# Quarter sums by block transposes and small products, in place of four full transposes, in layer 0 of a two-layer diffusion backbone

## The chip, the cores and the metric

The kernel runs on one core of a Trainium2 chip. The metric is the device time of one execution in microseconds; a time given for a kernel is the median of its runs.

## What is computed

Two layers of a diffusion backbone work on 256 latent tokens and 256 context tokens of width 2048. Layer 0 mixes tokens by centred pooling, layer 1 by neighbourhood attention; each is followed by a gated MLP of width 5504. Every sub-layer is normalised and then shifted, scaled and gated by vectors that come out of the conditioning:

```python
    silu_c, silu_cc = jax.nn.silu(c), jax.nn.silu(c_ctx)
    for i in range(DEPTH):
        ml = (silu_c @ w_mod[i] + b_mod[i]).reshape(B, 6, 1, D)
        mc = (silu_cc @ w_mod[i] + b_mod[i]).reshape(6, 1, 1, D)
        a_lat = modulate(rms_norm(h, norm1_g[i]), ml[:, 0], ml[:, 1])
        a_ctx = modulate(rms_norm(hc, norm1_g[i]), mc[0], mc[1])
        ...
        h = h + ml[:, 2] * y_lat
        h = h + ml[:, 5] * conv_ffn(modulate(rms_norm(h, norm2_g[i]), ml[:, 3], ml[:, 4]), ...)
```

`modulate(x, shift, scale)` is `x * (1 + scale) + shift`. The two streams, latent and context, are two columns beside each other wherever a vector of the conditioning is meant.

## The kernel before

Channels lie on the partitions, tokens along the free dimension, both streams beside each other (512 columns). Most products are in fp32r, with weights and activations split into a high and a low part, so that three products stand for one; those of the conditioning are plain fp32. The instructions are written in an order, and a scheduler with a simulated timeline then orders each engine's queue, by readiness and by the written order as priority; `tc.high_priority()` lifts what is written under it above its place. Each engine's queue is in order on the chip.

The conditioning of layer 0 (the modulation) is 24 chunks of 512 output channels. A chunk is the function `mod_pe`: in four steps it loads 1 MB of weights each, and multiplies them with the conditioning. The stationary operand is 32 columns wide (two hold the streams, the rest are zero), and four such products stand side by side in the column groups of the array (`tile_position`), each with another quarter of the contraction, into one PSUM bank, tag "m", of which there is one (L193). So the bank ends up with four partial sums, at partitions 0, 32, 64 and 96, two rows each, along 512 columns. They have to be added, and turned so that the channels lie on the partitions. Before, ScalarE copies the bank to SBUF (L198, "modev"), TensorE turns it by four full 128x128 transposes (L203, "modt", under high priority), and VectorE adds the four quarters with one reduction (L205); `by_row` is the view for that. `finish_mod` adds the bias (L181) and, for a scale, multiplies (L183).

The generator `mods` runs through the chunks, and `need(n)` drives it to step n. Between the steps, the mixer of the pooling layer and the early part of the MLP are written: `partial(g, ...)` multiplies the MLP's gate and up weights of the first eight blocks with the channel group g as soon as that group is through the mixer, on activations without the shift (L545 to L547). The part of the shift goes through the same weights separately: `pw` (L528) multiplies the unsplit weights with the shift `sh`, again with 32 columns in four column groups, in 16 units (four channel groups, two blocks of four, gate and up). Its bank is copied by ScalarE (L532, "peg" and "peu"), turned by four transposes (L561, "ptg" and "ptu") at the end of the unit, and reduced (L564, or L568 and an addition L569) into `wsh`.

`quad` is a matrix that sums four quarters of the partitions; layer 1's conditioning uses it in `quarter_sum` (L165), behind VectorE's block transposes (L251), which turn each 32x32 block of a tile in its place. Loads are issued on SP's queue into a ring of rooms of half a megabyte (L127); a room comes free when the last reader of its weights is done. The tiles of 512 columns share a ring of six, tag "t2"; PSUM banks of tag "d" are three.

Of the kernel before, what the change touches and what calls it, by code (L numbers as in the profile page):

```python
# [17 lines left out]
P = 128  # L18
# [39 lines left out]
def kernel(ctx: ExitStack, tc: tile.TileContext, xT, cxT, wmod, wg, wu, wd, wp,  # L58
# [10 lines left out]
    def bank(tag, name):  # L69

        if tag == "d" and nbank[0] is not None:
            nbank[0] += 1
            if nbank[0] % 4 == 0:
                tag = "m"
        return pp.tile([P, 512], F32, tag=tag, bufs={"gu": 4, "d": 3, "m": 1}[tag], name=name)
# [78 lines left out]

    both = (0, 1)

    def by_row(ps):

        return ps.rearrange("p (i j c) -> p i c j", i=4, j=4)[:, :, 0:2, :]

    def quarter_sum(x, n, name):

# [5 lines left out]

    def finish_mod(l, ch, streams, src):

        mt = src[0] if len(src) == 1 else main.tile([P, 4, 2], F32, name=f"modT{l}_{ch}")
        n = len(streams)
        which, q = divmod(ch, 4)

        def dup(name, a):
            return V(name)[:, a : a + 8].rearrange("p (i s) -> p i s", s=2)[:, :, 0:n]

        bias = dup(f"bm_{l}", 8 * ch)
        for b, v in enumerate(src):
            own = slice(32 * b, 32 * b + 32) if len(src) > 1 else slice(0, P)  # L180
            nc.vector.tensor_tensor(mt[own, :, 0:n], v, bias[own], op=ALU.add)  # L181
        if which in (1, 4):
            nc.vector.scalar_tensor_tensor(mt[:, :, 0:n], mt[:, :, 0:n], 1.0, dup(f"g{1 if which == 1 else 2}_{l}", 8 * q),  # L183
                                           op0=ALU.add, op1=ALU.mult)
        modT[l, ch] = mt

    def mod_pe(l, ch, sc, pool):

        ps = bank("m", f"mod{l}_{ch}")
        for g in range(4):  # L190
            ts = load(lambda a, b: wmod[l, ch, g, :, a:b], 2048, f"wm{l}_{ch}_{g}")
            for j in range(4):
                nc.tensor.matmul(ps[32 * j : 32 * j + 32, :], sc[:, 4 * g + j, :],  # L193
                                 ts[j // 2][0][:, 512 * (j % 2) : 512 * (j % 2) + 512],
                                 start=(g == 0), stop=(g == 3), tile_position=(0, 32 * j))
            if g == 3:
                ev = pool.tile([P, 512], F32, tag="t2", name=f"modev{l}_{ch}")
                nc.scalar.copy(ev, ps)  # L198
            yield
        with tc.high_priority():  # L200
            p2 = bank("d", f"modt{l}_{ch}")
            for i in range(4):
                nc.tensor.transpose(p2[:, P * i : P * i + P], ev[:, P * i : P * i + P], ident)  # L203
        r = main.tile([P, 4, 2], F32, name=f"modT{l}_{ch}")
        nc.vector.tensor_reduce(out=r, in_=by_row(p2), axis=AX.X, op=ALU.add)  # L205
        finish_mod(l, ch, both, [r])

    def mod_pairs(todo, ring):

# [113 lines left out]
    with ExitStack() as ph0:  # L323
# [62 lines left out]
        with ExitStack() as phs:  # L386
# [123 lines left out]
            def partial(g, sh, between):  # L510

                step = 0
                for fa in range(0, NS, 4):
                    for q, (nm, wsrc) in enumerate((("g", wg), ("u", wu))):
# [3 lines left out]
                        for j in range(4):  # L518
                            f = fa + j
                            between(2 * step)  # L520
                            if j == (3 if fa == 0 and q == 0 else 0):
                                need(20 * g + 21)
                                assert g in READY
                                pw = bank("d", f"pw{nm}{g}_{fa}")
                                for i in range(4):
                                    for jj, (t, n) in enumerate(ts):
                                        t3 = t.rearrange("p (f c) -> p f c", c=512)
                                        nc.tensor.matmul(pw[32 * i : 32 * i + 32, 256 * jj : 256 * jj + 256], sh[:, i, :],  # L528
                                                         t3[:, :, P * i : P * i + P], start=True, stop=True,
                                                         tile_position=(0, 32 * i))  # L530
                                ev = f0.tile([P, 512], F32, tag="t2", name=f"pe{nm}{g}_{fa}")
                                nc.scalar.copy(ev, pw)  # L532
                            if f >= NC:
                                if g == 0:
                                    HELD[f, q] = bank("gu", f"c{nm}_{f}")
# [20 lines left out]
                                nc.scalar.copy(PART[f][:, q], ps)  # L556
                            else:
                                nc.vector.tensor_tensor(PART[f][:, q], PART[f][:, q], ps, op=ALU.add)
                        p2 = bank("d", f"pt{nm}{g}_{fa}")
                        for i in range(4):  # L560
                            nc.tensor.transpose(p2[:, P * i : P * i + P], ev[:, P * i : P * i + P], ident)  # L561
                        w_ = wsh[:, q, fa : fa + 4, :]
                        if g == 0:
                            nc.vector.tensor_reduce(out=w_, in_=by_row(p2), axis=AX.X, op=ALU.add)  # L564
                            continue
                        t_ = f0.tile([P, 512], F32, tag="t2", name=f"pu{nm}{g}_{fa}")[:, 0:8]
                        t_ = t_.rearrange("p (f s) -> p f s", s=2)
                        nc.vector.tensor_reduce(out=t_, in_=by_row(p2), axis=AX.X, op=ALU.add)  # L568
                        nc.vector.tensor_tensor(w_, w_, t_, op=ALU.add)  # L569
            lend(range(4, KT))  # L570
            mix = mixer(0)
            for n in STEPS:
# [659 lines left out]
```

## Time and profile before

| | us |
|---|---|
| median of 3 runs | 3101.84 |
| lowest and highest | 3100.47, 3102.82 |
| the profiled execution | 3103.48 |
| its span, first to last instruction | 3101.7 |
| TensorE busy in the span | 3030.0 |
| VectorE busy | 1932.6 |
| ScalarE busy | 1373.2 |
| GpSimd busy | 826.1 |

The profile comes from one execution of its own, so its times are compared with that execution's. In its rows PE is TensorE's matmuls, PEld its weight loads, which overlap with them, DVE VectorE, ACT ScalarE, POOL GpSimd and SPq the queue that issues the loads. Matmuls overlap, so that their durations can't be added; the distance from start to start says what one takes of the engine. The early part that the change touches lies in the first 455 us.

### The profile page before, as it was taken

The page shows a single profiled execution, that of the slowest core. Times are in us where ns is not written, and L with a number is a line of the kernel's source. Part 1 is how long each engine was busy: PE and PEld are TensorE (multiplying, and loading weights), DVE is VectorE, ACT ScalarE, POOL GpSimd, SP SyncE. Part 2 cuts the span into 40 slices and gives each one's busy share as a digit, 9 for nine tenths or more (in the row PEclk, how much of TensorE's full clock was granted, in tenths as well). Part 3 has the DMA queues.
Part 4 walks back from the last instruction along what each step waited for, and adds up shares of the span by engine and source line. Part 5 has one row for each costly group of instructions (what it writes and reads, how often), then busy time and mean ns, then how long its engine had stood idle before and what let it go on. Part 6 is the DMA issues. An engine that isn't in the chain of part 4 may idle for free.

```text
span 3101.7 us, 40819 instructions
## 1 busy us (share of the span) xinstructions
PE 3030.0 (98%) x15082; PEld 2414.3 (78%) x15082; DVE 1932.6 (62%) x2748; ACT 1373.2 (44%) x2219; POOL 826.1 (27%) x823
## 2 busy tenths in 40 slices
PE   6999899999999999999999999999999999999998
PEld 2565558888888888888888788878788888888887
DVE  4445674285765848567485665564777666666666
ACT  3333454333233332323334444343545666656665
POOL 2011213213031230302213000000002466556665
PEclk9999999999999999999999999999999999999999
DMA  9978573264846657475573333332345565555563
GB/s 376 333 271 306 177 246 102 89 217 149 251 141 206 198 162 247 133 225 171 182 226 118 102 113 106 102 114 96 111 153 179 177 196 188 192 189 185 179 195 117
DMA packets 177927, 559.70 MB, mean 180 GB/s; under 512 B 17600, under 2 KB 22208, under 8 KB 177728
## 3 DMA queue, kind: packets, MB, share of 16 engines
q1 hardware_dynamic: 177728, 557.10, 55.0%
q8 instruction: 119, 1.95, 0.3%
q14 instruction: 80, 0.66, 0.1%
HBM read 554.93 MB, written 2.10 MB: 180 GB/s over the span
## 4 chain that ended last, share of the span: by engine, by line
PE 94%; DMA 2%; DVE 2%; POOL 1%; ACT 1%; issue 0%; SPq 0%; DVEq 0%; ACTq 0%; POOLq 0%
PE g L766 5%; PE u L766 5%; PE d L657 5%; PE d L659 5%; PE d L658 5%; PE d L813 4%; PE u L631 4%; PE u L632 4%; PE u L633 4%; PE g L631 4%; PE g L633 4%; PE g L632 4%; PE mod L193 3%; PE u L769 3%; PE g L769 3%; PE d L817 2%
## 5 line engine op out<-in xcount | busy, mean ns | idle before, releaser
L670 POOL TENSOR_TENSOR hl<-hl,dy 128x256 f32<-128x256 f32 x160 | 149.0, 931 | 958.6 <-ACT dy L669 957.3
L828 POOL TENSOR_TENSOR hl<-hl,dy 128x256 f32<-128x256 f32 x320 | 331.5, 1069 | 188.4 <-ACT dy L826 186.1
L241 DVE SCALAR_TENSOR_TENSOR macc<-wm,sc,macc 128x512 f32<-128x512 f32 (+1 forms) x360 | 325.2, 935 | 68.6 <-DMA wm<-wmod 67.6
L669 ACT ACTIVATE dy<-d,modT 128x256 f32<-128x256 f32 x320 | 133.5, 470 | 196.8 <-PE d L659 195.5
L193 PE MATMUL mod<-wm,sc 128*32 128x512 f32 x768 | 134.6, 618 | 26.6 <-DMA wm<-wmod 26.5
L670 POOL TENSOR_TENSOR hc<-hc,dy 128x256 f32<-128x256 f32 x160 | 126.0, 787 | 0.0
L145 DVE TENSOR_TENSOR wd_2l<-wd,wd_2h 128x1024 fp32r<-128x1024 f32 (+1 forms) x44 | 53.9, 1229 | 112.8 <-ACT wd_2h L143 112.8
L826 ACT ACTIVATE dy<-d,modT 128x512 f32<-128x512 f32 x160 | 104.4, 683 | 42.7 <-PE d L817 41.2
L915 POOL TENSOR_TENSOR rk<-rk,rp 128x256 f32<-128x256 f32 x16 | 13.2, 826 | 365.4 <-DVE rk L914 309.8
L145 DVE TENSOR_TENSOR wd_3l<-wd,wd_3h 128x1024 fp32r<-128x1024 f32 (+1 forms) x44 | 52.0, 1202 | 80.6 <-ACT wd_3h L143 80.6
L145 DVE TENSOR_TENSOR wd_1l<-wd,wd_1h 128x1024 fp32r<-128x1024 f32 (+1 forms) x44 | 53.7, 1224 | 58.6 <-ACT wd_1h L143 58.6
L466 POOL TENSOR_TENSOR pf<-ws,inv 128x256 f32<-128x256 f32 x32 | 27.7, 886 | 222.4 <-DVE ws L461 154.7
L193 PEld LDWEIGHTS mod<-wm,sc 128*32 128x32 f32 x768 | 23.6, 110 | 81.0 <-issue 59.4
L143 ACT CAST wd_1h<-wd 128x1024 fp32r<-128x1024 f32 (+1 forms) x44 | 45.2, 1029 | 79.8 <-PE u L632 50.6
L145 DVE TENSOR_TENSOR wd_0l<-wd,wd_0h 128x1024 fp32r<-128x1024 f32 (+1 forms) x44 | 54.6, 1247 | 40.7 <-ACT wd_0h L143 40.6
L1004 ACT ACTIVATE sb<-sb,nm 128x512 f32<-128x512 f32 x64 | 46.1, 721 | 64.4 <-DVE nm L1000 63.2
L143 ACT CAST wd_0h<-wd 128x1024 fp32r<-128x1024 f32 (+1 forms) x44 | 45.3, 1031 | 57.9 <-PE u L766 29.1
L792 DVE TENSOR_TENSOR actb<-sgb,actb 128x256 fp32r<-128x256 f32 x43 | 52.3, 1216 | 27.0 <-ACT actb L791 27.0
L657 PE MATMUL d<-act,wd_2h 128*128 128x512 f32 x172 | 68.0, 395 | 0.0
L658 PE MATMUL d<-act,wd_2h 128*128 128x512 f32 x172 | 67.9, 395 | 0.0
L657 PE MATMUL d<-act,wd_3h 128*128 128x512 f32 x172 | 67.9, 395 | 0.0
L657 PE MATMUL d<-act,wd_0h 128*128 128x512 f32 x172 | 67.9, 395 | 0.0
(1752 smaller groups left out, 9286.1 us busy)
## 6 DMA issues: line engine op xcount, KB each, us to landing
wm<-wmod SPq DMA_DIRECT2D x384, 512.0 KB, 6.1
wd<-wd SPq DMA_DIRECT2D x168, 512.0 KB, 4.4
wg<-wg SPq DMA_DIRECT2D x156, 512.0 KB, 4.6
wu<-wu SPq DMA_DIRECT2D x156, 512.0 KB, 4.5
wv<-wv SPq DMA_DIRECT2D x32, 512.0 KB, 3.9
wk<-wq SPq DMA_DIRECT2D x32, 512.0 KB, 4.0
wq<-wq SPq DMA_DIRECT2D x32, 512.0 KB, 3.7
wo<-wo SPq DMA_DIRECT2D x32, 512.0 KB, 4.4
```

What stands on the lines that cost most here:

```text
L145: eng.tensor_tensor(lo[:, :n], t[:, :n], hi[:, :n].bitcast(F32), op=ALU.subtract)
L193: nc.tensor.matmul(ps[32 * j : 32 * j + 32, :], sc[:, 4 * g + j, :], ts[j // 2][0][:, 512 * (j % 2) : 512 * (j % 2) + 512], start=(g == 0) ...
L241: nc.vector.scalar_tensor_tensor(acc[s], v, sc2[:, k, s : s + 1], acc[s], op0=ALU.mult, op1=ALU.add)
L631: nc.tensor.matmul(ps, hi[:, c : c + P], xh, start=(k == 0), stop=False)
L632: nc.tensor.matmul(ps, hi[:, c : c + P], xl, start=False, stop=False)
L633: nc.tensor.matmul(ps, lo[:, c : c + P], xh, start=False, stop=(k == KT - 1))
L657: nc.tensor.matmul(ps, hi[:, o : o + P], xh, start=(i == 0), stop=False)
L658: nc.tensor.matmul(ps, hi[:, o : o + P], xl, start=False, stop=False)
L670: nc.gpsimd.tensor_tensor(h_of(s)[:, k, :], h_of(s)[:, k, :], y[:, s], op=ALU.add)
L766: nc.tensor.matmul(ps, hi[:, c : c + P], flat(B[k]), start=(k == 0), stop=False)
L769: nc.tensor.matmul(ps[:, T:], lo[:, c : c + P], B[k][:, 0], start=False, stop=(k == KT - 1))
L828: nc.gpsimd.tensor_tensor(hl[:, k, :], hl[:, k, :], y[:, q], op=ALU.add)
```

## The change

The copy by ScalarE, the four full transposes and the reduction go. VectorE transposes the PSUM bank in blocks of 32x32 straight into an SBUF tile (`turned`). After that a column of the tile, within a block, holds one row of the bank, so the two rows that matter of every block are columns, with the channels of that block along 32 partitions, and the quarter of the contraction in the partition group. Four products with the first 32 columns of `quad` as the stationary operand, each with eight moving columns, add the quarters and put each of the four 32-channel blocks at its own partitions, side by side in the column groups of the array (`by_row`). `finish_mod` reads the PSUM bank directly. The products of the modulation are no longer under high priority. In the early shift sums the reduction with its extra tile goes too: the sum in PSUM is copied into `wsh` for the first channel group, and added for the others.

```diff
-    def by_row(ps):
-
-        return ps.rearrange("p (i j c) -> p i c j", i=4, j=4)[:, :, 0:2, :]
+    def turned(ps, pool, name):
+
+        t = pool.tile([P, 512], F32, tag="t2", name=name)
+        nc.vector.transpose(t, ps)
+        return t.rearrange("p (i b r) -> p b i r", b=4, r=32)[:, :, :, 0:2]
+
+    def by_row(x, name):
+
+        ps = bank("d", f"{name}s")[:, 0:8].rearrange("p (i s) -> p i s", s=2)
+        for b in range(4):
+            nc.tensor.matmul(ps[32 * b : 32 * b + 32], quad[:, 0:32], x[:, b], start=True, stop=True,
+                             tile_position=(0, 32 * b))
+        return ps
...
             if g == 3:
-                ev = pool.tile([P, 512], F32, tag="t2", name=f"modev{l}_{ch}")
-                nc.scalar.copy(ev, ps)
+                x = turned(ps, pool, f"modev{l}_{ch}")
             yield
-        with tc.high_priority():
-            p2 = bank("d", f"modt{l}_{ch}")
-            for i in range(4):
-                nc.tensor.transpose(p2[:, P * i : P * i + P], ev[:, P * i : P * i + P], ident)
-        r = main.tile([P, 4, 2], F32, name=f"modT{l}_{ch}")
-        nc.vector.tensor_reduce(out=r, in_=by_row(p2), axis=AX.X, op=ALU.add)
-        finish_mod(l, ch, both, [r])
+        finish_mod(l, ch, both, [by_row(x, f"modt{l}_{ch}")])
...
-                                ev = f0.tile([P, 512], F32, tag="t2", name=f"pe{nm}{g}_{fa}")
-                                nc.scalar.copy(ev, pw)
+                                x = turned(pw, f0, f"pe{nm}{g}_{fa}")
...
-                        p2 = bank("d", f"pt{nm}{g}_{fa}")
-                        for i in range(4):
-                            nc.tensor.transpose(p2[:, P * i : P * i + P], ev[:, P * i : P * i + P], ident)
-                        w_ = wsh[:, q, fa : fa + 4, :]
+                        w_, v = wsh[:, q, fa : fa + 4, :], by_row(x, f"pt{nm}{g}_{fa}")
                         if g == 0:
-                            nc.vector.tensor_reduce(out=w_, in_=by_row(p2), axis=AX.X, op=ALU.add)
-                            continue
-                        t_ = f0.tile([P, 512], F32, tag="t2", name=f"pu{nm}{g}_{fa}")[:, 0:8]
-                        t_ = t_.rearrange("p (f s) -> p f s", s=2)
-                        nc.vector.tensor_reduce(out=t_, in_=by_row(p2), axis=AX.X, op=ALU.add)
-                        nc.vector.tensor_tensor(w_, w_, t_, op=ALU.add)
+                            nc.vector.tensor_copy(w_, v)
+                        else:
+                            nc.vector.tensor_tensor(w_, w_, v, op=ALU.add)
```

## Rows read from the trace of the kernel before

**Rows 1.** The page: busy us of each engine, share, instructions.

```profile
PE 3030.0 (98%) x15082; PEld 2414.3 (78%) x15082; DVE 1932.6 (62%) x2748; ACT 1373.2 (44%) x2219; POOL 826.1 (27%) x823
```

**Rows 2.** Windows: length, busy PE, PEld, DVE, ACT, POOL; granted clock, DMA share, GB/s.

```profile
0.00:78.00 78.00, 48.20 (x209) 19.05 (x210) 31.15 (x59) 30.28 (x70) 16.49 (x31) 0.96 0.97 375
78.00:455.00 377.00, 363.87 (x1976) 212.53 (x1975) 206.87 (x363) 146.16 (x264) 60.46 (x61) 0.99 0.77 271
222.00:247.00 25.00, 23.56 (x133) 13.90 (x132) 24.83 (x42) 9.50 (x16) 6.02 (x6) 1.00 0.84 296
```

**Rows 3.** Waits of TensorE, 78 to 455 us: total us, times, longest.

```profile
PE pwu L528 <- DMA wcu<-wu: 5.4, 2, 4.1
```

**Rows 4.** Groups by line: busy us, mean ns of one, idle before and why.

```profile
L203 PE MATMUL modt<-ident,modev 128*128 128x128 f32 x96 | 15.2, 282 | 7.8 <-ACT modev L198 7.8
L198 ACT COPY modev<-mod 128x512 f32<-128x512 f32 x24 | 13.9, 580 | 60.7 <-PE mod L193 60.7
```

**Rows 5.** Timeline, TensorE at 89 us: start, us, instruction, idle before.

```profile
89.04 0.60 PE L203 MATMUL modt<-ident,modev 128*128 128x128 f32 x4
89.57 1.91 PE L193 MATMUL mod<-wm,sc 128*32 128x512 f32 x12
```

**Rows 6.** Timeline, TensorE at 138 us.

```profile
138.39 0.66 PE L561 MATMUL ptg<-ident,peg 128*128 128x128 f32 x4
138.98 0.88 PE L528 MATMUL pwu<-wcu,sh 128*32 128x256 f32 x12
```

**Rows 7.** Timeline, TensorE at 108 us.

```profile
107.69 0.39 PE L545 MATMUL cu<-Ad,wcu_0h 128*128 128x512 f32 x1
...
108.59 0.40 PE L547 MATMUL cu<-Ad,wcu_0l 128*128 128x512 f32 x1
```

**Rows 8.** Timeline, 75 to 78 us.

```profile
75.19 0.16 PEld L193 LDWEIGHTS mod<-wm,sc 128*32 128x32 f32 x8 [0.35 <-issue]
...
77.71 0.65 PE L203 MATMUL modt<-ident,modev 128*128 128x128 f32 x4 [1.45 <-ACT modev L198]
...
78.00 0.69 DVE L282 TENSOR_TENSOR n2acc<-n2acc,n2q 128x512 f32<-128x512 f32 x1 [2.11 <-ACT n2q L276]
```

**Rows 9.** Timeline, TensorE at 234 us.

```profile
234.17 0.66 PE L203 MATMUL modt<-ident,modev 128*128 128x128 f32 x4 [1.44 <-ACT modev L198]
```

**Rows 10.** Timeline, TensorE at 765 us: one product by the whole of `quad`.

```profile
765.02 0.29 PE L165 MATMUL modt_8s<-modr,quad 128*128 128x16 f32 x2
765.16 0.48 PE L632 MATMUL g<-A,wg_16h 128*128 128x512 f32 x1
```

**Rows 11.** Single lines: ns of one (least/median/most), first and last start.

```profile
L528 PEld LDWEIGHTS pwg<-wcg,sh x128: 106/110/110, 94.4 to 410.6; 128*32 128x32 f32 x128
L205 DVE TENSOR_REDUCE modT<-modt x24: 177/191/192, 33.1 to 453.3; 128x8 f32<-128x32 f32 x24
L251 DVE STREAM_TRANSPOSE modu<-macc x32: 665/686/708, 663.4 to 1687.5; 128x512 f32<-128x512 f32 x32
```

**Rows 12.** Timeline, TensorE at 443 us: into tiled products and back.

```profile
443.08 0.39 PE L547 MATMUL cu<-Ad,wcu_4l 128*128 128x512 f32 x1
443.40 1.06 PE L193 MATMUL mod<-wm,sc 128*32 128x512 f32 x8
444.40 0.50 PE L545 MATMUL cu<-Ad,wcu_4h 128*128 128x512 f32 x1
444.73 0.39 PE L546 MATMUL cu<-Ad,wcu_4h 128*128 128x512 f32 x1
```

**Rows 13.** Timeline, VectorE, 364 to 369 us.

```profile
364.58 1.63 DVE L310 SCALAR_TENSOR_TENSOR nrm<-hl,modT,n2acc 128x256 f32<-128x256 f32 x1
...
368.43 0.16 DVE L417 COPY sh<-modT 128x8 f32<-128x8 f32 x1
```

**Rows 14.** Timeline, TensorE at 369 us.

```profile
368.69 1.09 PE L528 MATMUL pwg<-wcg,sh 128*32 128x256 f32 x16 [1.56 <-ACT A L312]
```

**Rows 15.** Windows, as rows 2, behind the waits for DMA.

```profile
380.60:387.30 6.70, 3.41 (x18) 1.87 (x19) 1.98 (x2) 1.63 (x2) 0.00 (x0) 0.50 0.88 297
```

More of the change, by code (lines that the diff above doesn't have):

```diff
@@ L169, in finish_mod @@
     def finish_mod(l, ch, streams, src):
-        mt = src[0] if len(src) == 1 else main.tile([P, 4, 2], F32, name=f"modT{l}_{ch}")
+        mt = main.tile([P, 4, 2], F32, name=f"modT{l}_{ch}")
         n = len(streams)
```

## Prediction

> **What bounds the kernel now.** First I read the busy line of each engine: TensorE is busy 98% of the span, VectorE 62%, ScalarE 44% [rows 1]. Then the same by stage, because the edit touches only layer 0's first 455 us [rows 2]. Up to 78 us TensorE works 48.20 of 78.00 us while the DMA engines are 0.97 busy: the weights' arrival sets the pace there, and TensorE work removed is worth nothing. From 78 to 455 us TensorE is busy 363.87 of 377 us, so idle for 13. After 455 us nothing is edited, and it is busy 3030.0 - 48.2 - 363.9 = 2617.9 us of 2646.7 [rows 1, 2], so what is won or lost by then should reach the end unchanged. So: between 78 and 455 us a microsecond of TensorE counts fully, as long as no other engine is late. Last the waits of TensorE there: the longest is for DMA, 5.4 us in two pieces [rows 3]; in the whole kernel 7.8 us are for ScalarE's copy "modev" ahead of the transposes [rows 4].
>
> **Part 1: TensorE, transposes against products.** There are 40 groups of four transposes: 24 of the modulation (L203, 96 instructions [rows 4]) and 16 of the early shifts (L561: four channel groups, two blocks, gate and up). I price them by the advance from start to start, since matmuls overlap, and sort them by their neighbours, counted along the timeline; one row stands for each kind.
>
> A full-array fp32r product advances 0.23 us. *A*, 20 groups, stand between such a product and column-tiled fp32 products (L193 or L528): 89.04 to 89.57 is 0.53, the group's price [rows 5]. *B*, 7 groups, stand between two column-tiled runs: 0.59 from 138.39 to 138.98 [rows 6], and about 0.1 before it to run L193 out: 0.69. *C*, 5 groups, stand between full-array products: 107.69 to 108.59 for two products and a group, 0.90 less 0.46 is 0.44 [rows 7]. *D*, 4 groups, come after a wait of TensorE, as at 77.71 and 234.17 [rows 8, 9]; they precede L193 as those of A do, so 0.53. Three lie in the DMA-paced start, and one, the last, ahead of another wait: worth nothing.
>
> The new products are 128x32 by eight columns, four beside each other. The trace shows each fp32 product as two instructions (L528 for gate: 64 products, 128 instructions [rows 11]), so a group is eight, in two rounds of four. No row shows such a group. The bounds: eight weight loads of this shape, four column groups side by side, took 0.16 us in all [rows 8], and eight columns stream in next to no time, so 0.16 at least. Above, one full-array product of this kind (two instructions, 16 columns) advanced 0.14, from 765.02 to 765.16 [rows 10]; four such in series are 0.56. I take 0.25: two rounds, each of which needs its own weights, at 0.106 to 0.110 a load [rows 11], and a little for the last. It is nearer to the low end because the four loads of a round have the shape and the placement of the row at that end. On top comes the change of array form: from a full-array product to a tiled one 0.32 instead of 0.23 (443.08 to 443.40), and back 0.34 instead of 0.23 for the first product (444.40 to 444.73) with some 0.09 ahead of it: 0.09 in, 0.20 out [rows 12].
>
> So A costs 0.34 instead of 0.53, 0.19 x 20 = 3.8 us won; B 0.25 instead of 0.69, 0.44 x 7 = 3.1; C 0.54 instead of 0.44, 0.5 lost; D 0.25 instead of 0.53, 0.28 x 4 = 1.1. Sum 7.5 us. At 0.16 a group it is 36 x 0.09 more, 10.7; at 0.56 it is 36 x 0.31 less, 3.7 lost.
>
> The Trainium skill (TensorEngine Tiling (Array Packing), Instruction Overhead) speaks against it: a matmul of one free column costs as much as one of 60, about 60 cycles, and one should not take the tiling from a dimension that is already small. By that page eight instructions in series would be an estimated 0.20 us a group, and this part 9.3 us; no row before shows it.
>
> **Part 2: the eviction moves from ScalarE to VectorE.** Removed are 40 copies of 0.58 us on ScalarE (23 us, [rows 4]) and 36 small reductions of 0.19 on VectorE [rows 11]; added are 40 block transposes. Rows have them for SBUF input alone, 0.686 [rows 11]; ScalarE takes 0.58 for the same tile out of PSUM. I take 0.69, and 0.58 to 0.9 as bounds. The four first shift sums trade a reduction for a copy. VectorE gains 40 x 0.69 - 36 x 0.19 = 21 us of work. Over the stretch it has room, 206.87 us of 377 [rows 2]; where it has, this costs nothing. Queued behind the new transpose are the low-half subtractions, the partial sums and the mixer's steps; TensorE waits for these, and for bank m, which the next chunk needs back.
>
> From 222 to 247 us there is no cover: VectorE is busy 24.83 of 25.00 [rows 2], and TensorE already waits 1.44 at 234.17 for a copy queued on ScalarE behind work that waits for VectorE [rows 9]. Two or three new transposes there are some 2 us, which I count as lost. Where ScalarE's copy ended a wait (four times), the transpose is 0.11 longer: 0.3 lost.
>
> **Part 3: waits that go.** At 76.26 the last tiled product of a chunk is done; ScalarE's copy is there at 77.71, when TensorE has waited 1.45; VectorE was free for the 2.11 us up to 78.00 [rows 8]. Transposed there, the products could start near 76.95: 0.7 won, since this is the hand-over to the stretch where TensorE counts. At 363.76 a transpose group feeds a reduction, then an addition that stood behind two normalisation steps (the first took 1.63 us), then the copy of the shift (368.43), for which TensorE waited 1.56 at 368.69 [rows 13, 14]. With one step less in this row the addition can go ahead of them; I count half, 0.8 won. What is late next there is DMA: the loads for the next unit, 5.4 us of waits [rows 3], issued when rooms come free. They move with it, and I count nothing more.
>
> Dropping the priority moves the products behind whatever is written before them; their input is then older when TensorE comes to it. I count nothing. The instructions of the loads keep their place in SP's queue; nothing is moved past GpSimd's.
>
> **The sum.** 7.5 + 0.7 + 0.8 - 2.0 - 0.3 = 6.7, say 7 us. The profiled execution took 3103.48 us (span 3101.7, 1.8 around it), 1.64 above the median of the runs. 3103.48 - 7 = 3096.5, and against the median 3101.84 - 7 = 3094.8.
>
> **Rivals.**
> *VectorE becomes the late engine (slower).* Its queue is in order. A transpose put ahead of the chunk's last product holds all that is behind it, as ScalarE sat idle 60.7 us until that product [rows 4]; and one put late keeps bank m and the products waiting. For: VectorE at 55% from 78 to 455 us and full from 222 to 247 [rows 2]. Against: ScalarE's 60.7 us cost TensorE 7.8 [rows 4]. At 1 us for every second of the 36 groups it is 18 us against a gain of 7: 3101.8 + 11 = 3113. It decides from about 0.4 us a group. Beside this row-based case: the Trainium skill (same page, PSUM Bottleneck) says that PSUM eviction can become the limit once TensorE is faster, and to use both ScalarE and VectorE for it; this change goes to VectorE alone, the busier of the two. No row before settles it.
>
> *The products don't run side by side.* At 0.56 a group part 1 loses 3.7, the rest stands at -0.8: 3101.8 + 4.5 = 3106, not to be told from no change.
>
> *The stall at 368 to 386 goes too.* If the shift is ready early enough for rooms and loads to move by more than TensorE does, the waits of 1.56 and 5.4 us vanish [rows 3, 14], and with them the stretch at a granted clock of 0.50 (the 1.2 GHz level, after these waits for DMA), where 3.41 us of work took twice its time [rows 15]: 7 + 1.7 more, less the 0.8 already counted: 3101.8 - 15 = 3087.
>
> **How the numbers follow.** Forecast 0.58 (3094.8; alone 3090 to 3099, by the bounds 0.16 and about 0.35 a group); VectorE late 0.18; no side by side 0.12; stall gone 0.12. A measurement of this kernel can tell about 0.2%, 6.2 us, from no change: the line lies at 3095.6. Of the forecast's 0.58 some two thirds lie beyond it: faster 0.39 + 0.12 = 0.51. Slower is most of the first rival, 0.15. Same is the rest, 0.34. The range goes from the stall rival's end, 3086, to 3107, beyond the serial products.
>
> **What would show it.** Right: the eight products of a group start within 0.3 us; the next tiled product follows the last full-array one by some 0.57 instead of 0.76; TensorE's idle time between 78 and 455 us stays near 13 us; ScalarE loses 23 us and VectorE gains 21. Wrong: starts 0.07 apart; new waits of TensorE for the transposes; VectorE idle behind the chunk's last product while TensorE waits for a partial sum. It would also be wrong if the order of work in the unedited rest came out differently.

## The result, and the profile after

| | before | after |
|---|---|---|
| median, runs taken in turn | 3102.6 (22 runs) | 3106.85 (22 runs) |
| ratio, 95% interval | | 1.0015 [1.0008, 1.0021] |
| the profiled execution, its span | 3103.48, 3101.7 | 3107.22, 3105.4 |

The change makes the kernel 0.15% slower, some 4.5 us, where 7 us of gain were forecast. That is within the 0.2% that the prediction called no change, and in the other direction. What was forecast for the edited instructions came, and more; what was forecast for the time did not. The rows that show it:

The page's busy line (as [rows 1]): TensorE is 7 us lighter, ScalarE 21, VectorE 13 heavier.

```profile
PE 3022.8 (97%) x15242; PEld 2406.3 (77%) x15242; DVE 1945.7 (63%) x2752; ACT 1352.1 (44%) x2179; POOL 827.6 (27%) x823
```

Windows, columns as [rows 2]:

```profile
0.00:78.00 78.00, 47.25 (x218) 17.95 (x218) 33.12 (x60) 27.66 (x64) 17.08 (x31) 0.93 0.96 373
78.00:455.00 377.00, 352.57 (x2091) 202.79 (x2091) 216.23 (x362) 126.01 (x227) 61.15 (x62) 0.97 0.75 265
222.00:247.00 25.00, 21.37 (x125) 12.86 (x124) 24.70 (x41) 8.46 (x14) 6.79 (x7) 0.86 0.91 314
```

From 78 to 455 us TensorE is busy 352.57 us instead of 363.87, and idle 24 instead of 13. The granted clock falls from a mean of 0.99 to 0.97, and from 222 to 247 us from 1.00 to 0.86.

TensorE's timeline, the places that answer to [rows 5, 6]:

```profile
92.05 0.39 PE L549 MATMUL cg<-Ad,wcg_0l 128*128 128x512 f32 x1
92.37 0.25 PE L167 MATMUL modt_12s<-modev,quad 128*32 128x8 f32 x8
92.46 1.04 PE L203 MATMUL mod<-wm,sc 128*32 128x512 f32 x8
...
138.27 0.25 PE L167 MATMUL modt_9s<-modev,quad 128*32 128x8 f32 x8
138.35 1.04 PE L203 MATMUL mod<-wm,sc 128*32 128x512 f32 x8
```

The eight instructions of a group take 0.08 to 0.09 us from start to start (92.37 to 92.46, 138.27 to 138.35). From the last full-array product to the next tiled one it is 0.41 instead of 0.76, of which 0.32 is the entry into tiled products, paid anyway.

The block transposes out of PSUM (line, engine, operation, count; ns least/median/most; first and last start):

```profile
L160 DVE STREAM_TRANSPOSE modev<-mod x24: 700/716/719, 31.5 to 457.0; 128x512 f32<-128x512 f32 x24
L160 DVE STREAM_TRANSPOSE peg<-pwg x8: 703/716/717, 99.3 to 423.9; 128x512 f32<-128x512 f32 x8
```

Waits of TensorE from 78 to 460 us (as [rows 3]: total, times, longest):

```profile
PE pwu L531 <- DMA wcu<-wu: 5.0, 2, 3.6
PE modt_11s L167 <- DVE modev L160: 4.8, 1, 4.8
PE modt_10s L167 <- DVE modev L160: 3.6, 1, 3.6
PE cg L547 <- ACT wcg_0h L143: 1.9, 1, 1.9
```

Two long waits for VectorE are new. The first one, on both engines:

```profile
234.23 1.22 DVE L145 TENSOR_TENSOR wp2l<-wp,wp2h 128x1024 fp32r<-128x1024 f32 x1
235.37 0.71 DVE L160 STREAM_TRANSPOSE modev<-mod 128x512 f32<-128x512 f32 x1
...
236.22 0.29 PE L167 MATMUL modt_10s<-modev,quad 128*32 128x8 f32 x8 [3.63 <-DVE modev L160]
236.36 1.93 PE L203 MATMUL mod<-wm,sc 128*32 128x512 f32 x8
```

Chunk 10's last product was done near 226.9. Its transpose comes at 235.37, behind 8 us of the mixer's work that fills VectorE's queue, and TensorE stands from 232.59 to 236.22. Before, a copy on ScalarE stood there, and TensorE waited 1.44 [rows 9]. And behind this wait the clock is half; windows over the four half-clock stretches of after from 78 us on (before had one there, [rows 15]; each has one more in the first 78 us):

```profile
84.70:88.10 3.40, 3.40 (x8) 1.01 (x8) 2.31 (x3) 0.15 (x1) 0.00 (x0) 0.50 1.02 384
234.90:241.70 6.80, 5.47 (x51) 2.32 (x54) 6.80 (x15) 1.53 (x3) 2.48 (x3) 0.50 0.71 210
330.50:337.30 6.80, 6.07 (x45) 3.32 (x46) 6.77 (x15) 1.64 (x3) 2.07 (x3) 0.50 0.41 122
391.90:398.70 6.80, 6.24 (x23) 2.50 (x24) 1.82 (x2) 1.04 (x1) 0.00 (x0) 0.50 0.79 299
```

Each follows, or begins within, a wait: 1.93 us for ScalarE's cast up to 83.95, the two for VectorE, 3.59 for DMA up to 392.46. TensorE works 3.40 + 5.47 + 6.07 + 6.24 = 21.2 us at the 1.2 GHz level, against 3.41 before, and half of such time is lost: some 9 us more. It isn't the profiled execution alone: the median of the granted clock over all runs is 0.9895 after (22 runs) and 0.993 before (the runs beside the experiments).

**Where the time went.** Along TensorE's timeline up to the first product of the MLP's regular row (L631 before), the advance from each start to the next is booked to its kind, less the idle time ahead of the next; half of what is worked at a granted clock of 0.50 is booked apart. For the experiments, which are told below, the same:

| us | ahead of the first product | turning (transposes or small products) | modulation products | other products | idle | half clock | sum: first L631 product | rounds of the modulation: all, four wide, two wide |
|---|---|---|---|---|---|---|---|---|
| before | 19.7 | 21.4 | 125.6 | 260.0 | 23.2 | 4.6 | 454.5 | 260, 124, 108 |
| after | 18.4 | 5.6 | 121.0 | 264.3 | 36.8 | 13.1 | 459.2 | 265, 125, 106 |
| e8, before with one transpose | 19.2 | 7.9 | 129.9 | 263.8 | 27.1 | 3.8 | 451.7 | 271, 115, 132 |
| e9, after with products five times | 18.5 | 17.9 | 115.8 | 264.4 | 32.6 | 9.4 | 458.5 | 251, 135, 86 |
| e14b, before with half the loads | 19.1 | 20.8 | 111.8 | 254.4 | 22.0 | 3.8 | 431.9 | 236, 148, 36 |
| e14a, after with half the loads | 18.7 | 4.2 | 104.7 | 259.3 | 22.2 | 2.2 | 411.4 | 229, 157, 30 |
| e15a, after without mixer's lows | 19.0 | 5.5 | 119.8 | 262.7 | 31.5 | 7.0 | 445.4 | 260, 123, 115 |
| e19, after with filler | 18.7 | 13.4 | 118.5 | 264.5 | 29.8 | 7.9 | 452.8 | 262, 123, 109 |

Turning falls by 15.8 us, and modulation and start by 5.9 more; waits take back 13.6, the half clock 8.5, the other products 4.3: 454.5 to 459.2. From there to the end it is 2647.2 before and 2646.3 after, so what is lost by then is lost at the end, as the prediction had it. In the other executions of the table this rest spreads from 2644.9 (e9) to 2650.9 (e14a), so that sums a few us apart say little of the whole time. All this is of one execution each; those of e8 and e15a ran 3.4 and 5.2 us below the medians of their kernels, the others within 1.

The last column is how the modulation's products run. A round is a run of its instructions without another product between them, in which each starts within 0.15 us of the one before; with all four column groups it is four wide (rounds of one or three are in the sum alone). In the kernel before:

```profile
125.52 1.06 PE L193 MATMUL mod<-wm,sc 128*32 128x512 f32 x8
126.51 0.50 PE L545 MATMUL cg<-Ad,wcg_4h 128*128 128x512 f32 x1
...
128.10 1.05 PE L193 MATMUL mod<-wm,sc 128*32 128x512 f32 x4
129.08 0.50 PE L546 MATMUL cg<-Ad,wcg_4h 128*128 128x512 f32 x1
```

Eight instructions, two rounds of four, advance 0.99; four, two rounds of two, advance 0.98. A step's weights lie in two rooms, two column groups in each, and where the order takes one room without the other, half a step costs as much as a whole one. So TensorE's busy time is not a fixed amount of work, and a busy line of 100% there hides it. What splits a step is mostly the order of TensorE's queue, which is made before the run: 20 of the 96 steps have other products between their halves. Up to 355 us, where 10 of the 20 lie, no late load does it on the chip: counted in order, the loads of both halves had landed when the first half began, with at least one more to spare. After that the loads come close to their use, and it can't be told.

### The profile page after: what moved, and what is told of

Read it like the earlier page. It is cut to its first block, busy times and chain, and to the rows that moved or that the text cites. A ratio compares the mean times of both kernels' runs of the same rounds, so it can differ in the third digit from the quotient of the medians.

```text
span 3105.4 us, 41091 instructions
## 1 busy us (share of the span) xinstructions
PE 3022.8 (97%) x15242; PEld 2406.3 (77%) x15242; DVE 1945.7 (63%) x2752; ACT 1352.1 (44%) x2179; POOL 827.6 (27%) x823
## 4 chain that ended last, share of the span: by engine, by line
PE 91%; DVE 3%; DMA 2%; POOL 1%; ACT 1%; issue 1%; SPq 0%; DVEq 0%; ACTq 0%; POOLq 0%
PE g L762 5%; PE u L762 5%; PE d L653 5%; PE d L655 5%; PE d L654 5%; PE d L809 4%; PE u L627 4%; PE u L628 4%; PE u L629 4%; PE g L627 4%; PE g L629 4%; PE g L628 4%; PE g L765 3%; PE u L765 3%; PE mod L203 2%; PE d L813 2%
## 5 line engine op out<-in xcount | busy, mean ns | idle before, releaser
L143 ACT CAST wd_0h<-wd 128x1024 fp32r<-128x1024 f32 (+1 forms) x44 | 45.1, 1030 | 59.5 <-PE g L628 29.8
```

## Experiments

All times stand beside runs of the kernel before on the same chip, 3100.4 to 3101.5 us, and ratios are to these. The changed kernel was not run again beside them: its ratio of 1.0015 is what they are compared with. Any of these edits also changes the order that the scheduler makes.

**1. The two parts alone, and chunks 10, 11 and 16 the old way.** e1 takes the modulation's part of the change alone, e2 that of the early shifts alone. e3 is the changed kernel with chunks 10 and 11 evicted and turned the old way, e5 with 16 too:

```diff
+                if ch in (10, 11, 16):
+                    ev = pool.tile([P, 512], F32, tag="t2", name=f"modev{l}_{ch}")
+                    nc.scalar.copy(ev, ps)
+                else:
+                    x = turned(ps, pool, f"modev{l}_{ch}")
```

Expected: e1: 

> The changed kernel, but the early shift sums as they were before: copy on ScalarE, four transposes, reduction. Theory (the products win some 0.36 us a group on TensorE; what is lost comes from three of the modulation's chunks): the 16 shift sums' gain of about 6 us is missing and the stalls stay, so 3110 to 3114, and TensorE waits of several us for the block transposes of chunks 10 and 11 as in the changed kernel. Rival (the shift sums' transposes crowd VectorE and are to blame): faster than the changed kernel, 3100 to 3104, and no such waits.

e2: 

> The changed kernel, but the modulation as before. Theory: the gain of 16 groups, about 6 us, and none of the three stalls: 3095 to 3099. Rival (the shift sums are to blame): 3104 or more. Second rival (the order of the whole early part is reshuffled by any such edit, and its stalls come and go): anywhere from 3096 to 3110, with new stalls at other places.

e3: 

> The changed kernel, but chunks 10 and 11 of the modulation (gates of channel groups 2 and 3) go the way of before: ScalarE's copy, transposes under high priority, reduction. Theory: the waits at 236 and 331 us (3.6 and 4.8 us) and the two stretches of 6.8 us at half the clock behind them go, and 1 to 2 us of wait for ScalarE come back: 12 us less than the changed kernel, 3093 to 3097. Rival (VectorE is late everywhere, these two places only show it): the stalls move to other chunks, 3102 to 3107.

e5: 

> As e3_two_chunks_old, and chunk 16 (the second scale of channel group 0) goes the way of before as well. Theory: the scheduler puts the cast of the first early weights back ahead of most of the eight activations of the hand-over, the early products start near 81 instead of 84 us, and the half clock from 84.7 to 88.1 us goes: 3 to 5 us less than e3_two_chunks_old, 3088 to 3093. Rival (the hand-over is set by the arrival of the weights): within 1 us of e3_two_chunks_old.

Measured: e1 3116.49, ratio 1.0049 [1.0036, 1.0063]; e2 3103.62, 1.0007 [0.9998, 1.0015]; e3 3104.91, 1.0013 [1.0004, 1.0022]; e5 3104.22, 1.0010 [1.0001, 1.0018]. e1's sign was as expected, and it lost more than either range allowed. e2's loss can't be told from nothing; it fits only its second rival, the reshuffled order, whose range fits almost anything. e3 and e5 came out as their rivals had it. The parts lose 15 and 2 us alone and 4.5 together, so they don't add up. In e3 the waits of 3.6 and 4.8 us fell to 1.4 and 1.8 and the half clock at 235 us went, as meant; yet the total idle time stayed (36.5 in the same booking), with new waits of 1 to 3 us at other places, and e5 is much the same (34.5). By the ratios, curing single waits brings 1 to 2 us at most, which can't be told from nothing.

**2. Does TensorE's time count?** e8 is the kernel before with one transpose of four in each group, whose columns the reduction reads four times (the sums are not the right ones); e9 the changed kernel with each group's products five times over.

```diff
-            for i in range(4):
-                nc.tensor.transpose(p2[:, P * i : P * i + P], ev[:, P * i : P * i + P], ident)
+            nc.tensor.transpose(p2[:, 0:P], ev[:, 0:P], ident)
...
+REPEAT = 5
...
+        for _ in range(REPEAT):
+            for b in range(4):
+                nc.tensor.matmul(ps[32 * b : 32 * b + 32], quad[:, 0:32], x[:, b], start=True, stop=True,
...
```

Expected: e8: 

> The kernel before with three of the four full transposes of each of the 40 groups left out (the reduction reads the first transpose's 128 columns four times, so the vectors of the conditioning are not the right ones; the copy stays on ScalarE, every other instruction stays). TensorE loses about 0.4 us in 36 groups that stand behind 78 us, 12 to 14 us, with no new work on VectorE. If a microsecond of TensorE between 78 and 455 us counts fully, as the prediction had it: 3087 to 3091 us against 3101.5. If that stretch is paced by the loads and by the chain of VectorE and ScalarE, so that TensorE only waits elsewhere for what it is spared: 3097 to 3103.

e9: 

> The changed kernel with the four small products of each group issued five times over (the same result each time), which gives TensorE back about 0.32 us in each of 36 groups, some 12 us, and changes nothing on the other engines. If TensorE's time counts fully: 3106 + 10 to 12 = 3116 to 3118 us. If the stretch is paced by something else: 3105 to 3110, the added work going into the waits.

Measured: e8 3107.0, 1.0017 [1.0008, 1.0025]; e9 3105.64, 1.0016 [1.0007, 1.0025], against 1.0015 of the changed kernel. Taking 13.5 us of turning away gains nothing, with nothing put on VectorE: the time lies above both ranges. Giving 12.3 back costs nothing, as the second range had it. That is the forecast's premise, and it fell. The table says how: in e8 the modulation's rounds go from 260 to 271, those two wide from 108 to 132 (4.3 us), the other products cost 3.8 more and the idle time 3.9; in e9 all this runs backwards (251 rounds, 86 two wide, 4.2 less idle, 3.7 less at half clock). It is the order again: up to 355 us 16 steps are split by other products in e8 (before 10) and 6 in e9 (after 9), and counted as above the loads of both halves had landed in each.

e8's row from 78 to 455 us, to be read against [rows 2]: 3.6 us less busy, and the loads no faster (269 GB/s, before 271).

```profile
78.00:455.00 377.00, 360.29 (x1860) 202.16 (x1853) 206.15 (x364) 147.18 (x269) 58.32 (x61) 0.99 0.76 269
```

**3. Loads.** e14b is the kernel before, e14a the changed one, with the modulation's weights loaded for every second step only; the step between uses those of the step before it once more:

```diff
+            if g % 2 == 0:
                 ts = load(lambda a, b: wmod[l, ch, g, :, a:b], 2048, f"wm{l}_{ch}_{g}")
```

Expected: e14b: 

> The kernel before with half of layer 0's modulation weights not loaded: every second of the four steps of a chunk uses the weights of the step before it again (the vectors of the conditioning are not the right ones). 48 of the 131 MB that are loaded up to 455 us go; the engines' work stays. If loads pace the stretch from 78 to 455 us: 3080 to 3094 us. If the chain of VectorE and ScalarE does: 3093 to 3102, most of it from the first 78 us, which wait for loads anyway.

e14a: 

> The changed kernel with the same half of the modulation weights not loaded. To be read against the kernel before with half the loads. If loads were what kept TensorE's gain from counting: 6 to 12 us below that one. If the chain of VectorE and ScalarE keeps it: as much above it as the changed kernel is above the kernel before, 2 to 6 us.

Measured: e14b 3081.43, 0.9935 [0.9918, 0.9952]; e14a 3063.75, 0.9878 [0.9863, 0.9892]. With half the loads the change is worth 17.7 us, more than the 6 to 12 expected, and its sign is turned. Windows of the two (e14b first), 78 to 410 us:

```profile
78.00:410.00 332.00, 330.08 (x1832) 197.87 (x1833) 183.52 (x320) 127.06 (x232) 55.52 (x59) 1.00 0.49 164
```

```profile
78.00:410.00 332.00, 327.14 (x2038) 193.30 (x2036) 210.19 (x347) 119.41 (x214) 59.89 (x61) 1.00 0.51 169
```

The DMA engines are busy 0.5 instead of 0.77, TensorE hardly waits, the clock is whole; two-wide rounds fall from 108 and 106 to 36 and 30, in part by the edit itself, as half of the steps load nothing. Here TensorE bounds the stretch, and the gain at the end is no less than the 16.6 us of turning (20.8 to 4.2). VectorE's heavier queue costs little: the waits for a transpose are 1.0 and 2.5 us, on chunks 19 and 23. One thing this pair can't separate: the scheduler orders the queues by its own timeline of the loads, so with fewer loads the order changes as well as the chip's transfers.

**4. VectorE's queue.** Eight subtractions of 1.22 us make the low halves of the mixer's weights, ahead of the late transposes. e15b (kernel before) and e15a (changed) leave them out; the high half stands in.

```diff
-                        parts = ld(wp[g], f"wp{g}")
+                            hi = whp.tile([P, 1024], F32R, tag="wh", name=f"wp{g}h{j}")
+                            nc.scalar.copy(hi, t)
+                            parts.append((hi, hi))
```

Expected: e15b: 

> The kernel before with the eight subtractions left out that make the low halves of the mixer's weights (1.22 us of VectorE each, two per channel group, in the mixer's run up to its products; the high half stands in for the low one, TensorE's work stays, the mixer's output is not the right one). If VectorE's queue at the ends of the groups paces the stretch: 3093 to 3098 us. If loads do: 3099 to 3102.

e15a: 

> The changed kernel with the same eight subtractions left out. To be read against the kernel before without them. If VectorE's queue was what kept TensorE's gain from counting, the stalls at 235 and 330 us shrink by 2 us and more each, their half-clock stretches go, and the time is 4 to 10 us below that one. If loads kept it: 2 to 6 us above it.

Measured: e15b 3105.34, 1.0012 [1.0002, 1.0021]; e15a 3099.08, 0.9989 [0.998, 0.9998]. The kernel before gains nothing from 10 us less on VectorE (it is slower than either range); the changed one gains some 8 and stands 6.3 below its counterpart, as the first range had it. So in the changed kernel, and not before, VectorE's queue is late, as far as one pair shows it: chunk 10's wait falls from 3.6 to 1.1 us, 11's from 4.8 to 2.5.

Three runs try to have this with nothing left out. e7 puts these subtractions on GpSimd, e10 does so in e5, e18 does so with the weights loaded one block earlier:

```diff
-                        parts = ld(wp[g], f"wp{g}")
+                        parts = ld(wp[g], f"wp{g}", 1)
```

Expected: e7: 

> The changed kernel with the low halves of the mixer's four weight groups subtracted on GpSimd in place of VectorE (8 subtractions of 128x1024, some 8 us of VectorE's work, at 60 to 80 us, and near 227, 320 and behind). If VectorE's queue at the ends of the groups sets the new waits, the transposes at 235 and 330 us come some 2 us earlier and the stalls of 3.6 and 4.8 us shrink: 3098 to 3103 us. If loads and rooms set them: 3104 to 3107.

e10: 

> The changed kernel with chunks 10, 11 and 16 evicted and turned the old way, which was 3104.2 us, and with the mixer's low halves on GpSimd. If VectorE paces what was left of the waits at the hand-overs of the channel groups, this is the version that keeps TensorE's gain: 3092 to 3098 us. If loads and rooms pace them: 3101 to 3105.

e18: 

> The changed kernel with the mixer's weights loaded one block earlier (behind the third block of a group) and their low halves subtracted on GpSimd, which takes 2.4 us for what VectorE does in 1.22, but now ahead of their use. VectorE loses 10 us in the stretches where it is full, with nothing left out. If VectorE's queue is what gives the gain back: 3096 to 3101 us, as without these subtractions (3099). If GpSimd's share of the chain costs as much as it frees, or the earlier loads do: 3105 to 3115.

Measured: e7 3117.39, 1.0059 [1.0045, 1.0073]; e10 3113.7, 1.0041 [1.0028, 1.0053]; e18 3123.59, 1.0071 [1.0058, 1.0083]. All are worse, by 9 us and more than their counterparts, e18 by most, and above every range expected. In e7's trace GpSimd needs twice VectorE's 1.22 us:

```profile
L145 POOL TENSOR_TENSOR wp2l<-wp,wp2h x2: 2514/2526/2537, 236.1 to 245.0; 128x1024 fp32r<-128x1024 f32 x2
```

They stand ahead of the mixer's products. That points to a chain through these engines, not VectorE's sum alone, but the cause wasn't separated further; in e18 the wait for chunk 10 grew to 9.2 us.

**5. Order.** e16a (changed) and e16b (before) load the mixer's weights two blocks earlier; e17 is the changed kernel with the modulation two steps further ahead; e6 puts the transposes and their products under high priority.

```diff
-                    if i == 3:
+                    if i == 1:
                         parts = ld(wp[g], f"wp{g}")
...
-LEAD = 18
+LEAD = 20
...
-                x = turned(ps, pool, f"modev{l}_{ch}")
+                with tc.high_priority():
+                    x = turned(ps, pool, f"modev{l}_{ch}")
```

Expected: e16a: 

> The changed kernel with the mixer's weights loaded and split two blocks earlier (behind the second block of a group in place of the fourth), nothing else. Their two subtractions of 1.22 us, which stand in the full stretches of VectorE ahead of the transposes of chunks 10 and 11, move to where VectorE has room. If VectorE's queue at the ends of the groups gives back TensorE's gain: the stalls of 3.6 us at 236 and 4.8 us at 331 shrink by 2 us and more each, as without the subtractions, and the time is 3096 to 3101 us. If it is the loads alone, which keep their number and come earlier: 3104 to 3109.

e16b: 

> The kernel before with the same step of the mixer's weights moved two blocks earlier. If VectorE's queue matters only since the transposes moved to it: 3099 to 3104 us, no change. If the earlier weights are a gain by themselves, whatever turns the banks: as far below 3101.5 as the changed kernel with them is below 3106.

e17: 

> The changed kernel with the modulation written two of its steps further ahead of the early products (LEAD 20 in place of 18), so that the last products of chunks 10 and 11, their transposes and their loads come earlier against the mixer. If the order of the transposes against the mixer's work costs the gain: 3095 to 3102 us. If loads and rooms do, which have to come in the same number and earlier: 3104 to 3112, with new waits for DMA.

e6: 

> The changed kernel with the block transposes of the modulation and their products under high priority, as the four transposes of the kernel before were. In VectorE's queue chunk 10's transpose then stands one subtraction (1.22 us) earlier, chunk 11's two places; little else moves. If the dropped priority is what cost the gain: 3096 to 3101 us. If the work that is ahead in VectorE's queue costs it, whatever the priority: 3103 to 3107, with the stall at 236 us shorter by about 1.2 us.

Measured: e16a 3108.18, 1.0026 [1.0017, 1.0035]; e16b 3112.94, 1.0037 [1.0025, 1.0050]; e17 3111.35, 1.0039 [1.0026, 1.0051]; e6 3105.64, 1.0017 [1.0009, 1.0026]. The earlier weights cost the kernel before 12.6 us, where no change or a gain was expected, and the changed one, by the ratios, some 3; with them in both the change would have been a gain of 5. In e16a chunk 10's wait grew to 5.5 us and 11's fell to 3.4; in e17 chunk 10's fell to 1.5, and new waits, most of them for ScalarE ahead of the mixer's products and not for DMA as expected, took its place. e6 shortened chunk 10's wait by 1.6 us and lengthened 11's by 0.8, and the time is that of the changed kernel: the dropped priority has no part that can be measured.

The order is also a rival for the loss itself. Three edits of the kernel before that take work away or move a load, and put nothing on VectorE's late places, made it slower: e8 by 5.8 us, e15b by 3.8, e16b by 12.6. The changed kernel's 4.5 us are of the same size, and no run holds the order while the change is made.

**6. Waits or clock?** e19 is the changed kernel with four fp32 products of 128x512 more behind the last product of chunks 10 and 11, overwritten at once; they keep TensorE at work where it waited.

```diff
+        if warm is not None:
+            for _ in range(4):
+                nc.tensor.matmul(full, ident, warm, start=True, stop=True)
```

Expected: 

> The changed kernel with four products of 128x512 in fp32 more (some 3.6 us of TensorE, their result is overwritten) behind the last product of each of chunks 10 and 11, so that TensorE works through most of the time in which it waited for their transposes (3.6 us at 236, 4.8 us at 331), and the rest comes no earlier. If the wait itself is the loss: 3105 to 3108 us, the work only filling it. If the half-clock stretches behind these two waits (6.8 us each) are part of the loss, they go, and the time falls by 3 us for each: 3099 to 3102. If TensorE's time counts: 3110 and more.

Measured: 3101.94, 1.0003 [0.9994, 1.0011]: more work for TensorE, and the changed kernel's loss is gone but for what can't be told from nothing, within the range that had the half clock as a part of it. Its windows at the two places:

```profile
222.00:247.00 25.00, 25.00 (x147) 14.76 (x147) 23.84 (x40) 8.89 (x14) 5.61 (x6) 1.00 0.89 315
315.00:345.00 30.00, 30.00 (x163) 17.05 (x162) 27.27 (x44) 8.97 (x14) 6.30 (x8) 1.00 0.67 234
```

The changed kernel's, the first as above:

```profile
222.00:247.00 25.00, 21.37 (x125) 12.86 (x124) 24.70 (x41) 8.46 (x14) 6.79 (x7) 0.86 0.91 314
315.00:345.00 30.00, 25.22 (x140) 15.53 (x139) 28.04 (x46) 8.88 (x15) 6.31 (x8) 0.89 0.67 240
```

With the filler (227.18 to 230.81) TensorE doesn't wait and the clock stays whole: in the booking the turning, which holds the filler, rises by 7.8, idle falls by 7.0 and half clock by 5.2; over all 11 runs the median of the granted clock is 0.992 instead of 0.9895. The two half-clock stretches, (5.47 + 6.07) / 2 = 5.8 us in the changed kernel, are gone; the time at the end falls by near 4. The pair doesn't separate the filler from the order: chunk 10's small products now start at 239.06, behind the shift's unit that followed them before, while VectorE's transpose came no earlier (235.87, after 235.37); and the half clock at 84.7 went too, where nothing was filled. So the half clock behind the two waits is a part of the loss, by these rows; how much of the 4 us is its own isn't shown.

## Why the prediction was wrong

**The premise was the step that failed:** "between 78 and 455 us a microsecond of TensorE counts fully, as long as no other engine is late". It was read from the busy line, 363.87 of 377 us. e8 and e9 show that it doesn't hold with these loads, e14 that it holds with half of them. The row was true and the reading wrong: the busy time was taken as a fixed amount of work, but 108 of the 260 rounds of the modulation were two wide, and with the order they become 132 (e8) or 36 (half the loads). In the changed kernel they hardly moved (106). There the condition failed too, "as long as no other engine is late": 21.7 us were won in the booking, and waits (13.6), half clock (8.5) and other products (4.3) took more than that back, where the sum had 2.0 and 0.3 for all of it. The DMA share of 0.77 in the same row [rows 2] was read as room. It is a mean: the kernel before, 120 to 150 us,

```profile
120.00:150.00 30.00, 30.00 (x157) 16.72 (x156) 19.51 (x35) 11.86 (x21) 6.15 (x8) 1.00 1.02 395
```

has TensorE at 30.00 of 30 us and the DMA engines full. TensorE itself waits for no load in this kernel from 78 us until 373; what the loads do to the stretch before that, they do through the other engines or the scheduler's order.

**Part 1** had the right sign and half the size: 7.5 us forecast, 15.8 booked (over all 40 groups; the way back into full-array products is booked to the other products). The term that was off is the group's price, 0.25 assumed and 0.08 to 0.09 measured, below even the lower bound of 0.16; with 0.085 the prediction's own sum is 7.5 + 36 x 0.165 = 13.4. That bound took the row of eight weight loads as time that the engine needs alone; after's weight-load queue shows that the next run's loads begin while these last:

```profile
92.37 0.16 PEld L167 LDWEIGHTS modt_12s<-modev,quad 128*32 128x32 f32 x8 [0.35 <-issue]
92.43 0.16 PEld L203 LDWEIGHTS mod<-wm,sc 128*32 128x32 f32 x8
```

The eight run side by side, and the rival of serial products is out. The Trainium skill's figure (TensorEngine Tiling (Array Packing), Instruction Overhead), an estimated 0.20 for eight in series, is not borne out by these rows either.

**Part 2.** The transposes cost 0.716 out of PSUM, near the 0.69 assumed. The 40 transposes sum to 28.5 us and the 40 reductions that went to 7.4, the 21 more that were forecast; the busy line rose by 13 only, as other instructions of VectorE came out shorter. The place was named rightly, 222 to 247 us without cover, but priced at 2 us in all: the waits there and at 331 us are 8.4 instead of the 1.44 of before, and the clock behind them was not priced at all.

**Part 3.** The 0.7 us of the hand-over at 77 turned into a loss: the early products start at 83.95 instead of 81.0, behind a wait of 1.93 for ScalarE, whose cast of their weights now stands behind all eight activations:

```profile
82.47 0.49 ACT L505 ACTIVATE Ad<-hc,modT 128x256 fp32r<-128x256 f32 x1
82.87 1.98 ACT L143 CAST wcg_0h<-wcg 128x1024 fp32r<-128x1024 f32 x2
```

That is the last condition of the prediction, the order of unedited work coming out differently. The 1.56 us wait at 368 did go, and the waits for DMA behind it stayed (5.0 instead of 5.4), as said. "I count nothing" for the priority stands by e6.

**Rivals.** VectorE late was the right mechanism as far as e15a shows it. It was priced at 1 us on every second group. It came instead as two long waits, with the half clock behind each, and a spread of small ones; and it decides only together with the loads, since e14a, with the same work on VectorE, loses nothing. The Trainium skill (TensorEngine Tiling (Array Packing), PSUM Bottleneck) says that PSUM eviction may limit once TensorE is faster; the waits of 3.6 and 4.8 us for transposes out of PSUM agree. The stall at 368 to 386 did not go.

**Left open:** how much of e14's effect is the transfers and how much the order that the scheduler makes of them (up to 355 us the landing times speak for the order where steps are split); how much of the loss is VectorE's waits and how much any new order would have cost; whether steps that are forced to run four wide would free the gain with all loads, which wasn't tried. No version that computes everything beat the kernel before: e2 and e19 can't be told from it.

## What to carry to other kernels

A full busy line proves that an engine is occupied, not that it is the bound: look whether its instructions run at their full width, and whether it is the queue's order or a late input that keeps them from it, and test it with one run that takes a known amount of its work away and one that gives it back. Price a new wait on TensorE with the half-clock stretch behind it. An edit that makes an engine earlier changes the static order of everything around it, and that can be worth more than the edit, either way (e16: 12.6 and some 3 us lost by the same line).

## What was not expected of the hardware

- Eight tiled fp32 instructions of 128x32 by eight columns advance TensorE by 0.08 us, less than one weight load of that shape lasts (0.106 to 0.110, [rows 11]).
- A block transpose of 128x512 takes 0.716 us out of PSUM and 0.686 out of SBUF.
- The granted clock is 0.50 (the 1.2 GHz level) behind a wait of 1.93 us in after (84.7 to 88.1), though not behind one of 1.94 at the same place in e19, and falls within a longer one (234.9, in a wait from 232.59 to 236.22); in e19 it stayed whole where the longer ones had been, with TensorE kept at work.
- A VectorE step of 128x256 takes 0.48 us at 224.30 and 0.96 at 229.12, while GpSimd works from 228.29 on; it wasn't tested by itself. Of the 32 such steps (L456) in after, the 12 beside no GpSimd work took 0.45 to 0.49 us, and the 16 with more than 0.5 us of it beside them 0.60 to 1.00. Timelines of after, VectorE and GpSimd:

```profile
224.30 0.48 DVE L456 SCALAR_TENSOR_TENSOR py<-hc,modT,rs 128x256 f32<-128x256 f32 x1
...
229.12 0.96 DVE L456 SCALAR_TENSOR_TENSOR py<-hl,modT,rs 128x256 f32<-128x256 f32 x1
...
228.29 2.38 POOL L469 TENSOR_TENSOR pf<-ws,inv 128x256 f32<-128x256 f32 x2 [55.33 <-DVE ws L464]
```
